# One level of Strassen's algorithm in both products of an FFN (hybrid decoder block, one Trainium2 core)

## The chip, the core and the metric

The kernel runs on one core of a Trainium2 chip. The core has TensorE (PE, matrix products, with PEld for its weight loads), VectorE (DVE), ScalarE (ACT), GpSimd (POOL) and SyncE (SP, which here issues every DMA). They run side by side, each through a queue of its own in a fixed order, and wait for one another by semaphores. SBUF is the working memory of 128 partitions; PSUM holds the sums of matmuls in eight banks of 128 x 512 float32. The metric is the device time in microseconds of one execution; lower is better.

## The reference

One layer of a hybrid decoder block on 1024 tokens of width 1024, with 16 meta tokens ahead of them, all in float32. Three mixers (sliding-window attention, forgetting attention, a gated recurrence) are merged and added to the residual `h`; the FFN follows. The change concerns the last four lines alone:

```python
u = rms_norm(h, norm_mix[l])
proj = u @ w_in[l]
...
merged = (g[:, :, 0] * (o_a @ w_branch[l, 0])
          + g[:, :, 1] * (o_f @ w_branch[l, 1])
          + g[:, :, 2] * (o_c @ w_branch[l, 2]))
h = h + merged @ w_out[l]
u = rms_norm(h, norm_ffn[l])
gate_ff, up_ff = jnp.split(u @ w_ffn_in[l], 2, axis=-1)      # 1024 -> 2 x 2816
h = h + (jax.nn.silu(gate_ff) * up_ff) @ w_ffn_out[l]        # 2816 -> 1024
return rms_norm(h, norm_final)[:, N_META:]
```

## The kernel before

Every large product is made of float32r matmuls in three passes. A float32 operand is split into a high part (`hi`, a copy on ACT into float32r) and the rest (`lo`, a subtraction on DVE): `split`, L115 to L124. `mm3` (L143) then multiplies hi by hi, hi by lo and lo by hi into one bank, so each 128 x 128 x 512 step is three matmuls.

The kernel is written with a tile framework. It finds the dependences between tiles by itself and sets the waits; a pool's `bufs` says how many tiles of a tag live at once, and a new tile of the tag waits until an old one is no longer read. A planner sets the order of the instructions on each engine ahead of time: of those that are ready in its model of the run it takes the one written first.

The projections, the mixers and their merging run first. Then the loop at L851 makes, for each half `c` of the tokens (512 tokens), `h` after the mixers (kept in DRAM as `h1s`), its norm, and by transposes on TensorE (L873) the feature-major split tiles `u2[c][k]` for the eight k-tiles of 128 features.

The FFN (L880 on) goes through its 22 feature tiles of 128 in pairs `f0`. For each tile the weights of gate and up are loaded and split (`load_w`, L126: `wr` to `wh` and `wl`), and for each token half two banks, `mm_g` and `mm_u`, are filled over eight k-tiles (L906). ACT takes the sigmoid (L909), DVE multiplies gate, sigmoid and up (L910, L911) and the product `sg` is split into `hl` (L912). The two rows of `w_ffn_out` are loaded (`for`) and split into `fh` and `fl` (L917). Then the pair is multiplied into the output: for each of the eight token tiles and each half of the 1024 columns, six matmuls into a bank (`tr_fo` or `sc_fo`, L932), which DVE adds to `acc[tt]` in SBUF (L936). So the second product follows each pair of feature tiles at once. With the last pair the sum of squares (L940), the gain on POOL (L943), the final norm (`finish`, L889, with `rstd_from`, L175) and the output follow tile by tile.

Of the kernel before, what the change touches and what calls it, by code (L numbers as in the profile page):

```python
# [16 lines left out]
P = 128  # L17
D = 1024
# [33 lines left out]
def hybrid_block(ctx, tc, h_in, w_in, w_v0, w_v1, w_bd, par, rows, gains, relt, onehot,  # L52
# [19 lines left out]
    pad(cp, 128)  # L72
# [70 lines left out]
    def mm3(ps, terms):  # L143

        n = 3 * len(terms)
        cost = ps.shape[-1] / 2.4 + 3
        i = 0
        for ah, al, bh, bl in terms:
            for a, b in ((ah, bh), (ah, bl), (al, bh)):
                pe.matmul(ps, a, b, start=i == 0, stop=i == n - 1)  # L150
                i += 1
            yield 3 * cost
# [602 lines left out]
    mp = ctx.enter_context(tc.tile_pool(name="m4", bufs=16, side="left", reuse_waits="tile"))  # L755
    bp = ctx.enter_context(tc.tile_pool(name="b4", bufs=8, side="right", reuse_waits="tile"))

    def hl_tile(pl):

        t = pl.tile([P, D], F32R, tag="m4", name=nm("hl"))  # L760
        return t[:, :512], t[:, 512:]

# [59 lines left out]
    mt = [[None] * KT for _ in range(2)]  # L822
    u2 = [[], []]
    with tc.tile_pool(name="r4", bufs=1, side="right", reuse_waits="tile") as r4:
# [26 lines left out]
        with tc.tile_pool(name="r4b", bufs=1, side="right", reuse_waits="tile") as r4b:  # L851
            for c in range(2):
                u2[c] = [hl_tile(mp if c else bp) for k in range(KT)]
                for tt in range(4 * c, 4 * c + 4):
# [14 lines left out]
                    for half in range(2):  # L869
# [4 lines left out]
                        for i in range(4):  # L874
                            k = 4 * half + i
                            split(u2[c][k][0][:, q], u2[c][k][1][:, q], pt[:, i * P:(i + 1) * P],
                                  part[:, P_NF + k:P_NF + k + 1])


    with tc.tile_pool(name="r5", bufs=1, side="right", reuse_waits="tile") as r5:  # L880
        acc = []
        for tt in range(8):
            a = r5.tile([P, D], F32, name=f"acc{tt}")
            dma(a, h1s[tt])
            acc.append(a)
        gfc = r5.tile([P, D], F32, name="gfc")
        dma(gfc, gains[1:2].partition_broadcast(P))

        def finish(tt, q, o):  # L889

            r = rstd_from(q, P)
            act.activation(o[0], o[0], AF.Copy, scale=r)
            dve.tensor_scalar(o[1], o[1], r, None, ALU.mult)  # L893
            for half in (1, 0):
                dma(out[tt * P:(tt + 1) * P, 512 * half:512 * half + 512], o[half])

        fin = {}
        for f0 in range(0, NF, 2):
            fow, at_ = [], []
            for f in range(f0, f0 + 2):  # L900
                w = [load_w(w_fi[f + NF * i], D) for i in range(2)]
                at_.append([hl_tile(mp) for c in range(2)])
                for c in range(2):
                    pg, pv = (mm_bank(f"_{x}{f}") for x in "gu")
                    for ps, (wh, wl) in zip((pg, pv), w):
                        run(mm3(ps, [(wh[:, k * P:(k + 1) * P], wl[:, k * P:(k + 1) * P], *u2[c][k])  # L906
                                     for k in range(KT)]))
                    sg = r5.tile([P, 512], F32, tag="sg", bufs=2, name=nm("sg"))
                    act.activation(sg, pg, AF.Sigmoid)  # L909
                    dve.tensor_tensor(sg, pg, sg, ALU.mult)  # L910
                    dve.tensor_tensor(sg, pv, sg, ALU.mult)  # L911
                    split(*at_[-1][c], sg)  # L912
                raw = wp.tile([P, D], F32, tag="wr", name=nm("for"))
                dma(raw, w_fo[f * P:(f + 1) * P])
                fh = r5.tile([P, D], F32R, tag="fh", bufs=3, name=nm("fh"))
                fl = r5.tile([P, D], F32R, tag="fl", bufs=3, name=nm("fl"))
                split(fh, fl, raw)  # L917
                fow.append((fh, fl))
            for tt in range(8):
                c, t0 = tt // 4, (tt % 4) * P  # L920
                q = slice(t0, t0 + P)
                last = f0 == NF - 2
                cols = [slice(0, 512), slice(512, D)]
                if last and tt == 7:
                    cols[1:] = [slice(512, 768), slice(768, D)]
                if last:
                    fin[tt] = (cp.tile([P, len(cols)], F32, tag=f"sf{len(cols)}", bufs=2, name=nm("sf")),
                               [r5.tile([P, 512], F32, tag="o", bufs=6, name=nm("o")) for _ in range(2)])
                for i, n in enumerate(cols):
                    w = n.stop - n.start  # L930
                    ps = (tr_bank, sc_bank)[i % 2](f"_fo{f0}")[:, :w]
                    run(mm3(ps, [(at_[i][c][0][:, q], at_[i][c][1][:, q], fow[i][0][:, n], fow[i][1][:, n])  # L932
                                 for i in range(2)]))
                    if last and tt > 0 and i == 1:
                        finish(tt - 1, *fin[tt - 1])
                    dve.tensor_tensor(acc[tt][:, n], ps, acc[tt][:, n], ALU.add)  # L936
                    if last:
                        sums, o = fin[tt]
# [82 lines left out]
```

## Time and profile before

| | us |
|---|---|
| median of 3 runs | 1741.51 (1741.38 to 1741.55) |
| the profiled execution | 1742.17 |
| its span, first to last instruction | 1740.4 |
| FFN in that span, first `mm_g` to last matmul | 1009.0 to 1729.75 |

How to read the rows that follow. The page's first part gives busy time, share of the span and number of instructions for each engine. A row of the windows view is one stretch of time: its length, the busy time of PE, PEld, DVE, ACT and POOL with instruction counts, the granted TensorE clock (1.00 is full speed), the share of the DMA engines in use and GB/s. A row of the groups view has line, engine, operation, what is written from what, partitions x elements and count, then the busy time in us and the mean length of one in ns, then the idle time before it and who ended it. A row of the timeline or of the chain of work begins with its start and length in us. Matmuls overlap in the pipeline, so the length of one is longer than the distance between two.

### The profile page before, as it was taken

What the parts mean: (1) busy time and instruction counts of PE and PEld (TensorE: products, weight loads), DVE (VectorE), ACT (ScalarE), POOL (GpSimd) and SP (SyncE); (2) the same over time, 40 slices, a digit from 0 to 9 for tenths busy, and PEclk for the clock granted to TensorE, in tenths of its full rate; (3) what the DMA queues carried; (4) which work ended last, traced back from release to release, by engine and by line L of the source; (5) the groups of instructions that cost most, each with busy time, mean ns of one, the idle gap of its engine ahead of it and who ended that gap; (6) DMA issues with size and microseconds to landing.
All of it is one profiled execution on the core that took longest, in us unless ns stands there. A gap on an engine that the chain in (4) does not pass through costs nothing.

```text
span 1740.4 us, 22250 instructions
## 1 busy us (share of the span) xinstructions
PE 1710.8 (98%) x8537; PEld 1443.1 (83%) x8537; DVE 865.9 (50%) x1746; ACT 647.2 (37%) x1228; POOL 192.4 (11%) x188
## 2 busy tenths in 40 slices
PE   7999999999999999999999999999999999999997
PEld 6898878888888888888878888888888888888885
DVE  6466565554666666513384344434434434434435
ACT  6455565554555555523364331211211211211214
POOL 2111011011222222102240000000000000000004
PEclk9999999999999999999999999999999999999999
DMA  7223242332432323197462241211211211211202
GB/s 259 67 94 109 103 126 98 104 100 70 140 103 73 121 68 111 61 325 261 139 224 97 85 169 37 73 37 37 73 37 37 73 37 37 73 37 37 73 12 97
DMA packets 70122, 170.35 MB, mean 98 GB/s; under 512 B 7416, under 2 KB 19016, under 8 KB 69760
## 3 DMA queue, kind: packets, MB, share of 16 engines
q1 hardware_dynamic: 70016, 168.93, 28.9%
q8 instruction: 67, 1.10, 0.3%
q14 instruction: 39, 0.32, 0.1%
HBM read 123.08 MB, written 40.49 MB: 94 GB/s over the span
## 4 chain that ended last, share of the span: by engine, by line
PE 85%; DVE 6%; issue 4%; ACT 2%; DMA 2%; POOL 1%; SPq 0%; POOLq 0%; DVEq 0%; ACTq 0%
PE mm_w L150 23%; PE mm_g L150 14%; PE mm_u L150 14%; PE sc_fo L150 6%; PE tr_fo L150 6%; PE mm_br L150 5%; PE mm_wo L150 5%; PE ob L547 3%; PE tr L558 3%; PE mm_v L150 2%; PE sc L632 1%; PE sc L633 1%; DVE o L893 1%; DVE x L400 1%; DVE wl L119 1%
## 5 line engine op out<-in xcount | busy, mean ns | idle before, releaser
L150 PE MATMUL mm_w<-uh,wh 128*128 128x512 f32 (+2 forms) x744 | 292.4, 393 | 0.0
L150 PE MATMUL mm_w<-uh,wl 128*128 128x512 f32 (+2 forms) x744 | 280.6, 377 | 0.0
L150 PE MATMUL mm_w<-ul,wh 128*128 128x512 f32 (+2 forms) x744 | 279.7, 376 | 0.0
L150 PE MATMUL mm_g<-hl,wh 128*128 128x512 f32 x704 | 217.0, 389 | 0.0
L150 PE MATMUL mm_u<-hl,wh 128*128 128x512 f32 x704 | 216.7, 389 | 0.0
L119 DVE TENSOR_TENSOR wl<-wr,wh 128x1024 fp32r<-128x1024 f32 x85 | 105.0, 1235 | 165.7 <-ACT wh L118 165.4
L118 ACT ACTIVATE wh<-wr 128x1024 fp32r<-128x1024 f32 x85 | 90.2, 1061 | 217.2 <-PE mm_g L150 81.9
L150 PEld LDWEIGHTS mm_w<-uh,wl 128*128 128x128 f32 x744 | 139.9, 188 | 25.5
L150 PEld LDWEIGHTS mm_g<-hl,wh 128*128 128x128 f32 x704 | 132.2, 188 | 27.6
L150 PEld LDWEIGHTS mm_u<-hl,wh 128*128 128x128 f32 x704 | 132.0, 188 | 27.3
L150 PEld LDWEIGHTS mm_w<-uh,wh 128*128 128x128 f32 x744 | 140.4, 189 | 12.7
L150 PEld LDWEIGHTS mm_w<-ul,wh 128*128 128x128 f32 x744 | 140.7, 189 | 11.7
L150 PE MATMUL mm_g<-hl,wl 128*128 128x512 f32 x352 | 136.9, 389 | 0.0
L150 PE MATMUL mm_u<-hl,wl 128*128 128x512 f32 x352 | 136.9, 389 | 0.0
L909 ACT ACTIVATE sg<-mm_g 128x512 f32<-128x512 f32 x44 | 26.0, 591 | 288.2 <-PE mm_g L150 288.2
L150 PE MATMUL tr_fo<-fh,hl 128*128 128x512 f32 (+1 forms) x356 | 123.5, 388 | 0.0
L150 PE MATMUL sc_fo<-fh,hl 128*128 128x512 f32 (+1 forms) x352 | 122.3, 388 | 0.8 <-DVE re L183 0.8
L150 PE MATMUL mm_br<-o,wh 128*128 128x512 f32 x384 | 118.3, 389 | 0.0
L119 DVE TENSOR_TENSOR pl<-tr,ph 128x384 fp32r<-128x384 f32 (+2 forms) x160 | 87.4, 555 | 47.1 <-ACT ph L118 43.1
L943 POOL TENSOR_TENSOR o<-acc,gfc 128x512 f32<-128x512 f32 x15 | 19.4, 1316 | 796.3 <-DVE acc L936 791.3
L911 DVE TENSOR_TENSOR sg<-mm_u,sg 128x512 f32<-128x512 f32 x44 | 30.4, 692 | 148.1 <-PE mm_u L150 148.1
L118 ACT ACTIVATE ph<-tr 128x384 fp32r<-128x384 f32 (+2 forms) x160 | 76.9, 486 | 52.9 <-PE tr L558 50.8
(207 smaller groups left out, 3161.3 us busy)
## 6 DMA issues: line engine op xcount, KB each, us to landing
wr<-w_in_dram SPq DMA_DIRECT2D x45, 512.0 KB, 3.7
wr<-w_fi_dram SPq DMA_DIRECT2D x44, 512.0 KB, 3.5
gz<-z SPq DMA_DIRECT2D x48, 256.0 KB, 2.1
o<-osp SPq DMA_DIRECT2D x24, 512.0 KB, 5.6
sg<-gz SPq DMA_DIRECT2D x48, 256.0 KB, 3.2
for<-w_fo_dram SPq DMA_DIRECT2D x22, 512.0 KB, 3.4
wb<-w_br_dram SPq DMA_DIRECT2D x24, 256.0 KB, 4.2
k<-k SPq DMA_DIRECT2D x20, 260.0 KB, 3.6
```

The costliest lines, as they stand in the source:

```text
L118: act.activation(hi, src, AF.Copy)
L119: i = dve.tensor_tensor(lo, src, f32(hi), ALU.subtract)
L150: pe.matmul(ps, a, b, start=i == 0, stop=i == n - 1)
L400: dve.tensor_tensor_scan(hs, r, g, 0.0, ALU.mult, ALU.add)
L547: pe.matmul(ob[:, q0:q0 + b - a], vt[:, c], x[:, a:b], start=count == 0, stop=count == n_mm - 1, skip_group_check=True)
L558: pe.transpose(tb[:, col:col + P], src, ident)
L632: pe.matmul(sc[:, :n], qs, kh[:, k0:k0 + n], start=True, stop=False)
L633: pe.matmul(sc[:, :n], qs, kl[:, k0:k0 + n], start=False, stop=True)
L893: dve.tensor_scalar(o[1], o[1], r, None, ALU.mult)
L909: act.activation(sg, pg, AF.Sigmoid)
L911: dve.tensor_tensor(sg, pv, sg, ALU.mult)
L943: pool.tensor_tensor(g, acc[tt][:, n], gfc[:, n], ALU.mult)
```

## The change

Strassen's algorithm, in Winograd's form, computes a 2 x 2 block product with 7 block products in place of 8, with sums of blocks as operands and of the products.

In the first product the blocks are: of the weights, gate and up of a feature tile by the two halves of the k-tiles (`a11`, `a12`, `a21`, `a22`); of the activations, the two halves of the k-tiles by the two token halves (`b11` to `b22`, now pairs of k-tiles in one tile). The sums of activations, T1 to T4, are made once by `combine()`; the sums of weights are made for each tile on POOL. Tile 0 is still computed by eight products (`swiglu_plain`). Some products are added onto a bank that holds an earlier one (`first=False`), after that one has been read.

In the second product the blocks are: token halves by feature tiles 0 to 10 and 11 to 21; and these by column halves of `w_ffn_out`. The first stage therefore takes tiles `j` and `j + 11` together, makes the sums on POOL (`combine_w`, `combine_a`) and writes the operands of the seven products to DRAM (`asp`, `bsp`). A second stage reads them back, splits them and runs the seven products one after the other, each over four banks.

```diff
-    def mm3(ps, terms):
+    def mm3(ps, terms, first=True):
...
-                pe.matmul(ps, a, b, start=i == 0, stop=i == n - 1)
+                pe.matmul(ps, a, b, start=first and i == 0, stop=i == n - 1, skip_group_check=not first)
...
+    def pair_tile(pl, **kw):
+        return [pl.tile([P, D], F32R, tag="m4", name=nm("pt"), **kw).rearrange("p (k t) -> p k t", k=2)
+                for a in range(2)]
...
-        for f0 in range(0, NF, 2):
...
-            for tt in range(8):
...
+        def product(ps, a, b, first=True):
+            run(mm3(ps, [(a[:, 0, k * P:(k + 1) * P], a[:, 1, k * P:(k + 1) * P],
+                          b[k // 2][0][:, k % 2], b[k // 2][1][:, k % 2]) for k in range(4)], first))
+
+        def operand(pl, tag, bufs, src):
+            t = pl.tile([P, 2, 512], F32R, tag=tag, bufs=bufs, name=nm(tag))
+            split(t[:, 0], t[:, 1], src)
+            return t
...
+        def swiglu(f, w, bb):
+            (a11, a12), (a21, a22) = w
+            b11, b21, b22, t1, t2, t3, t4 = bb
+            p1, p2, p5 = mm_bank(f"_s{f}"), sc_bank(f"_s{f}"), tr_bank(f"_s{f}")
+            g0, g1, u1 = (t5("c", 8) for _ in range(3))
+            s0, s1 = (t5("a", 6) for _ in range(2))
+            s2 = t5("s2", 2)
+            product(p1, operand(wp, "wh", 2, a11), b11)
+            act.activation(g0, p1, AF.Copy)
+            product(p2, operand(wp, "wl", 2, a12), b21)
+            add(dve, g0, p2, g0)
+            act.activation(s0, g0, AF.Sigmoid)
+            dve.tensor_tensor(s0, g0, s0, ALU.mult)
+            sub(pool, a21, a11, a21)
+            sub(pool, s2, a22, a21)
+            product(p1, operand(r5, "ar", 3, s2), t2, False)
+            act.activation(g1, p1, AF.Copy)
+            add(pool, a11, s2, a11)
+            product(p5, operand(r5, "ar", 3, a11), t1)
+            act.activation(u1, p5, AF.Copy)
+            product(p1, operand(r5, "ar", 3, a21), t3, False)
+            add(dve, u1, p1, u1)
+            sub(pool, a12, a12, s2)
+            product(p5, operand(wp, "wh", 2, a12), b22, False)
+            add(dve, g1, p5, g1)
+            act.activation(s1, g1, AF.Sigmoid)
+            dve.tensor_tensor(s1, g1, s1, ALU.mult)
+            dve.tensor_tensor(s1, u1, s1, ALU.mult)
+            product(p1, operand(wp, "wl", 2, a22), t4, False)
+            dve.tensor_tensor(s0, p1, s0, ALU.mult)
+            return [s0, s1]
+
+        def combine():
+            b11, b21 = u2[0][:2], u2[0][2:]
+            b12, b22 = u2[1][:2], u2[1][2:]
...
+            for k in (0, 2, 1, 3):
+                e = pool if k > 1 else dve
+                v3, v2[k] = t5("c", 8), t5("c", 8)
+                for v, x, y in zip((v3, v2[k]), parts(b22, k), parts(b12, k)):
+                    sub(e, v, x, y)
+                add(e, v3, v3, v2[k])
+                for x, y in zip((v3, v2[k]), parts(b11, k)):
+                    add(e, v2[k], x, y)
+                into(t2, k, v2[k])
+                into(t3, k, v3)
+            t4 = [pair_tile(mp) for _ in range(2)]
+            for t, b in ((t1, b22), (t4, b21)):
+                for k in (0, 2, 1, 3):
+                    e = pool if k > 1 else dve
+                    v = t5("c", 8)
+                    h, l = parts(b, k)
+                    sub(e, v, h, v2[k])
+                    add(e, v, v, l)
+                    into(t, k, v)
+            return b11, b21, b22, t1, t2, t3, t4
...
+        def combine_w(j):
+            raws = []
+            for i in range(2):
+                raw = t5("fo", 2, D)
+                dma(raw, w_fo[(j + NJ * i) * P:(j + NJ * i + 1) * P])
+                raws += halves(raw)
+            b11, b12, b21, b22 = raws
+            t2 = t5("t2", 1)
+            sub(pool, b12, b22, b12)
+            add(pool, t2, b12, b11)
+            sub(pool, b11, b22, t2)
+            sub(pool, b21, b21, t2)
+            for i, x in ((2, t2), (3, b11), (4, b12), (6, b21)):
+                dma(bsp[i][j], x)
+
+        def combine_a(j, a11, a21, a12, a22):
+            s2 = t5("t2", 1)
+            spill(1, j, a12)
+            spill(6, j, a22)
+            sub(pool, a21, a11, a21)
+            sub(pool, s2, a22, a21)
+            add(pool, a11, s2, a11)
+            sub(pool, a12, a12, s2)
+            for i, x in ((2, s2), (3, a11), (4, a21), (5, a12)):
+                spill(i, j, x)
+
+        for j in range(NJ):
+            if j == 0:
+                first = swiglu_plain(0)
+                ws = fetch_fi(NJ, 0)
+                bb = combine()
+            else:
+                first = swiglu(j, fetch_fi(j, 1), bb)
+                ws = fetch_fi(j + NJ, 0)
+            spill(0, j, first[0])
+            combine_w(j)
+            combine_a(j, *first, *swiglu(j + NJ, ws, bb))
...
+        def operands(i, j):
+            raw = wp.tile([P, 2, 512], F32, tag=("wr", "wh", "wl")[j % 3], bufs=2, name=nm("raw"))
+            dma(raw[:, 0], asp[i][j])
+            dma(raw[:, 1], right_operand(i, j))
+            t = rr.tile([P, 2, 2, 512], F32R, tag="ab", bufs=15, name=nm("ab"))
+            split(t[:, 0], t[:, 1], raw)
+            return t[:, 0], t[:, 1]
+
+        def product2(i, banks, first=True, by_token=None):
...
+            if by_token is None:
+                for j in range(NJ):
+                    ops = {j: operands(i, j)}
+                    for x in range(4):
+                        mm(x, ops, [j])
+            else:
+                ops = [operands(i, j) for j in range(NJ)]
+                for x in range(4):
+                    mm(x, ops, range(NJ))
+                    by_token(x)
...
+        product2(0, yb)
...
+        ho = [[h_tile(tt, half) for half in range(2)] for tt in range(8)]
+        for x in range(4):
+            add(dve, ho[x][0], yb[x], ho[x][0])
+        product2(1, xb)
...
+        product2(5, xb, False)
+        for x in range(4):
+            add(dve, ho[x][1], xb[x], ho[x][1])
+            total(x, 1)
+            finish(x)
+
+        def last(x):
+            add(dve, ho[4 + x][0], yb[x], ho[4 + x][0])
+            total(4 + x, 0)
+            finish(4 + x)
+        product2(6, yb, False, last)
```

`swiglu_plain` is the old loop's first product for one tile; `fetch_fi` loads the weights of gate and up without splitting them, into two buffers of one of two pools by turns; `spill` writes an operand to `asp`; `mm` in `product2` issues three matmuls for each `j` into the bank of token tile `x`; `total` and `finish` take the sum of squares, the norm and the output of a token tile.

More of the change, by code (lines that the diff above doesn't have):

```diff
@@ L71, in hybrid_block @@
     pad(edge, LINE - 32)
-    pad(cp, 128)
+    pad(cp, 192)
     ctxu = ctx.enter_context(ExitStack())
@@ L754, in hybrid_block @@
     ctxu.close()
-    mp = ctx.enter_context(tc.tile_pool(name="m4", bufs=16, side="left", reuse_waits="tile"))
-    bp = ctx.enter_context(tc.tile_pool(name="b4", bufs=8, side="right", reuse_waits="tile"))
+    ctx4 = ctx.enter_context(ExitStack())
+    mp = ctx4.enter_context(tc.tile_pool(name="m4", bufs=16, side="left", reuse_waits="tile"))
+    bp = ctx4.enter_context(tc.tile_pool(name="b4", bufs=8, side="right", reuse_waits="tile"))
     def hl_tile(pl):
@@ L852, in hybrid_block @@
             for c in range(2):
-                u2[c] = [hl_tile(mp if c else bp) for k in range(KT)]
+                u2[c] = [pair_tile(mp if c else bp) for k in range(KT // 2)]
                 for tt in range(4 * c, 4 * c + 4):
@@ L875, in hybrid_block @@
                             k = 4 * half + i
-                            split(u2[c][k][0][:, q], u2[c][k][1][:, q], pt[:, i * P:(i + 1) * P],
+                            split(*(x[:, k % 2, q] for x in u2[c][k // 2]), pt[:, i * P:(i + 1) * P],
                                   part[:, P_NF + k:P_NF + k + 1])
-    with tc.tile_pool(name="r5", bufs=1, side="right", reuse_waits="tile") as r5:
-        acc = []
-        for tt in range(8):
[L883 to L886, printed above, removed]
-        dma(gfc, gains[1:2].partition_broadcast(P))
[L889 to L897, printed above, removed]
-        for f0 in range(0, NF, 2):
[L899 to L938, printed above, removed]
-                        junk = r5.tile([P, 512], F32, tag="jk", bufs=2, name=nm("jk"))
-                        act.activation(junk[:, :w], acc[tt][:, n], AF.Square, accum_out=sums[:, i:i + 1])
-                        g = o[n.start // 512][:, n.start % 512:n.start % 512 + w]
-                        if w == 512:
-                            pool.tensor_tensor(g, acc[tt][:, n], gfc[:, n], ALU.mult)
-        for n in cols[1:]:
-            tc.keep_in_program_order(dve.tensor_tensor(o[1][:, n.start - 512:n.stop - 512], acc[7][:, n],
-                                                       gfc[:, n], ALU.mult))
-        finish(7, *fin[7])
```

88 lines of the change are left out of this document (added).

## The prediction

> **What bounds the kernel now.** I read the page's busy times first, then the busy time by stage for the FFN, then the groups of TensorE there, and last the chain of work.
>
> ```profile
> PE 1710.8 (98%) x8537; PEld 1443.1 (83%) x8537; DVE 865.9 (50%) x1746; ACT 647.2 (37%) x1228; POOL 192.4 (11%) x188
> 1009.00:1729.90 720.90, 719.95 (x3183) 595.44 (x3181) 292.47 (x398) 134.81 (x203) 16.13 (x13) 1.00 0.17 57
> L150 PE MATMUL mm_g<-hl,wh 128*128 128x512 f32 x704 | 217.0, 389 | 0.0
> L150 PE MATMUL mm_u<-hl,wh 128*128 128x512 f32 x704 | 216.7, 389 | 0.0
> L150 PE MATMUL mm_g<-hl,wl 128*128 128x512 f32 x352 | 136.9, 389 | 0.0
> L150 PE MATMUL mm_u<-hl,wl 128*128 128x512 f32 x352 | 136.9, 389 | 0.0
> L150 PE MATMUL tr_fo<-fh,hl 128*128 128x512 f32 x352 | 122.6, 389 | 0.0
> L150 PE MATMUL sc_fo<-fh,hl 128*128 128x512 f32 x348 | 121.4, 389 | 0.2 <-DVE re L183 0.2
> L150 PE MATMUL tr_fo<-fl,hl 128*128 128x512 f32 x176 | 68.5, 389 | 0.0
> L150 PE MATMUL sc_fo<-fl,hl 128*128 128x512 f32 x174 | 67.7, 389 | 0.0
> ...
> 1075.53 5.44 PE mm_g L150 x24
> ...
> 1140.81 5.44 PE mm_g L150 x24
> ```
>
> In the FFN (1009.0 to 1729.9 us) TensorE is busy 719.95 of 720.90 us while DVE needs 292 and ACT 135: TensorE alone sets the end. The groups give 2112 matmuls for the first product and 1050 full ones for the second, and twelve half-width ones make up the other 6: 3168 in all. The 389 ns are latencies of overlapping matmuls; the pace is the chain's, 24 in 5.44 us, **0.2267 us** each. A pair of feature tiles (288 matmuls) repeats after 1140.81 - 1075.53 = 65.28 us, the same pace, so there is no hole between groups. Full-width work is 3168 x 0.2267 = 718 us.
>
> **What the change removes.** A Strassen step does a feature tile's gate and up for both token halves in 7 products of 4 k-tiles x 3 passes, 84 matmuls, where the old loop has 2 x 2 x 8 x 3 = 96. Tile 0 stays plain: 96 + 21 x 84 = 1860, 252 fewer. The second product is 7 x 11 x 4 x 3 = 924 for 1056, 132 fewer. Together 384 x 0.2267 = **87.0 us**.
>
> The end of the old loop goes too.
>
> ```profile
> 1729.47 0.28 PE L150 MATMUL tr_fo<-fh,hl 128*128 128x256 f32 x1
> 1734.37 0.41 DVE L936 TENSOR_TENSOR acc<-tr_fo,acc 128x256 f32<-128x256 f32 x1
> 1734.88 0.42 ACT L940 ACTIVATE jk<-acc 128x256 f32<-128x256 f32 x1 [0.57 <-DVE acc L936]
> 1736.33 0.49 DVE L893 TENSOR_SCALAR o<-o,rs 128x512 f32<-128x512 f32 x1
> 1736.38 0.72 ACT L892 ACTIVATE o<-o,rs 128x512 f32<-128x512 f32 x1 [0.28 <-DVE rs L185]
> L873 PE MATMUL tr<-ident,xg 128*128 128x128 f32 x8 | 1.1, 276 | 0.0
> L119 DVE TENSOR_TENSOR hl<-sg,hl 128x512 fp32r<-128x512 f32 x44 | 30.3, 689 | 15.4 <-ACT hl L118 15.4
> L911 DVE TENSOR_TENSOR sg<-mm_u,sg 128x512 f32<-128x512 f32 x44 | 30.4, 692 | 148.1 <-PE mm_u L150 148.1
> L118 ACT ACTIVATE hl<-sg 128x512 fp32r<-128x512 f32 x44 | 27.5, 625 | 124.4 <-DVE sg L911 124.4
> L119 DVE TENSOR_TENSOR wl<-wr,wh 128x1024 fp32r<-128x1024 f32 x42 | 51.5, 1225 | 93.4 <-ACT wh L118 93.4
> L118 ACT ACTIVATE wh<-wr 128x1024 fp32r<-128x1024 f32 x42 | 44.6, 1063 | 162.7 <-PE mm_g L150 81.9 <-PE mm_u L150 80.8
> L943 POOL TENSOR_TENSOR o<-acc,gfc 128x512 f32<-128x512 f32 x15 | 19.4, 1316 | 796.3 <-DVE acc L936 791.3 <-issue 3.0 <-DMA out_dram<-o 1.0
> ```
>
> The last matmul ends at 1729.75 and the span at 1740.4: a tail of 10.65 us, since DVE had a backlog and reached the last bank 4.6 us late. Now each of the last four token tiles has 33 matmuls (7.5 us) to be finished under. Of the last one stands: the add 0.7, the square 0.6, from its end to the scaling about 1.0 (1734.88 + 0.42 to 1736.33), two scalings at 0.7, and the 3.3 us from the last scaling's end (1737.10) to the span's end: about 6.9, **3.8 us saved**. PE's old holes in the last groups were 720.75 - 718 - about 0.8 for the eight transposes, **1.8 us**, and go. With nothing added the span is 1740.4 - 87.0 - 3.8 - 1.8 = **1647.8**.
>
> **What it adds, stage by stage.** *First product, steady state.* A tile is 84 matmuls, 19.0 us. On ACT 7 hi halves, 3 bank copies and 2 sigmoids, about 12 x 0.6 = 7 us; on DVE 7 lo halves and 7 bank or gating operations, 14 x 0.69 = 9.7; on POOL 4 sums per tile and 8 more per pair for the second product's operands, 8 x 1.32 = 10.5. None reaches 19.0. New is that a product adds onto a bank which ACT or DVE is still to read (`first=False`): one product (2.72 us) always lies between, against a copy of 0.6 or an add of 0.7, so 2 us of queue in front of them are covered.
>
> But POOL and DVE are not independent.
>
> ```profile
> 905.10 2.86 POOL L843 TENSOR_TENSOR sg<-sg,macc 128x512 f32<-128x512 f32 x2 [3.30 <-DVE sg L842]
> 905.47 0.69 DVE L842 TENSOR_TENSOR sg<-mm_br,sg 128x512 f32<-128x512 f32 x1
> 907.41 1.10 DVE L119 TENSOR_TENSOR hl<-sg,hl 128x512 fp32r<-128x512 f32 x1 [1.25 <-ACT hl L118]
> 911.90 1.29 POOL L843 TENSOR_TENSOR sg<-sg,macc 128x512 f32<-128x512 f32 x1 [0.42 <-DVE sg L842]
> 912.51 1.23 DVE L119 TENSOR_TENSOR hl<-sg,hl 128x512 fp32r<-128x512 f32 x1 [0.69 <-ACT hl L118]
> ```
>
> DVE's lo half at 907.41 takes 1.10, not 0.69: POOL ends at 907.96, and 0.55 us later DVE ends too. At 912.51 again: POOL ends at 913.19, DVE at 913.74. DVE's read of a bank (905.47) isn't held up. So where both of DVE's inputs lie in SBUF it waits for POOL, and holds it off for some 0.55 us itself. [...]
>
> In a pair that is 16 POOL operations x 1.29 = 20.6 us and 20 such DVE ones (14 lo halves, 6 gatings) x 0.55 = 11.0: 31.6 of 38.1 us. It fits; bounds 0 and 20 us for the whole loop (the upper end worked out in the rivals). A product's DVE work is about two operations, 1.4 us, and 2.7 with a whole POOL operation ahead, just under its 2.72; so near the lower end: **3 us**.
>
> *The start.* `combine()` builds T1 to T4 from u2.
>
> ```profile
> 1018.37 0.61 DVE L124 SCALAR_TENSOR_TENSOR hl<-tr,part,hl 128x128 fp32r<-128x128 f32 x2 [0.18 <-ACT hl L123]
> ```
>
> u2 is whole at 1019.0. TensorE is covered by the plain tile until 1009.0 + 21.8 + 0.8 = 1031.6 and by the two products that need no T until 1037.0. T2 and T3 take 10 operations on POOL and 10 on DVE plus 8 lo halves. If the POOL ones and as many of DVE's alternate, 10 x (1.29 + 0.55) = 18.4, and the last split 1.3 and a wait: ready about 1040, 3 us late. T1 (4 and 4 operations, 7.4, its split behind) comes at 1046 against 1042.7: 4 us more. T4 at 1054 is just in time. If POOL and DVE didn't hold each other up, POOL's 10 x 1.29 would end at 1032 and nothing would wait; if all 42 us of port time (18 x 1.29 + 34 x 0.55) with DVE's bank work stood in line, some 18 are lost. Bounds 0 and 18; from the rows above I take **8 us**.
>
> ```profile
> 1732.00:1733.00 1.00, 0.00 (x0) 0.00 (x0) 0.54 (x3) 0.97 (x4) 1.00 (x2) 0.99 1.04 401
> 1733.00:1734.00 1.00, 0.00 (x0) 0.00 (x0) 1.00 (x2) 1.00 (x4) 1.00 (x1) 0.50 0.15 55
> 760.00:780.00 20.00, 20.00 (x90) 16.56 (x89) 1.86 (x2) 4.99 (x8) 0.00 (x0) 1.00 0.91 326
> for<-w_fo_dram SPq DMA_DIRECT2D x22, 512.0 KB, 3.4
> gz<-z SPq DMA_DIRECT2D x48, 256.0 KB, 2.1
> 914.90 0.33 SPq L58 DMA_DIRECT2D for<-w_fo_dram  x1
> ```
>
> The granted clock falls to 0.50 some 3.2 us after the last matmul, so a stall beyond that is paid with slow matmuls too; how long they stay slow no row shows. [...]
>
> *The DRAM path.* A pair loads 6 x 512 KB and spills 11 x 256 KB, 5.9 MB in 38.1 us, 154 GB/s; the second stage reads 512 KB per 12 matmuls (2.72 us), 193 GB/s. At 760 us the kernel moves 326 GB/s with TensorE fully busy, so both fit, with a landing of 2 to 4 us under six raw buffers (16 us ahead). In the second stage a step needs ACT 1.06 and DVE 1.23 of 2.72, and POOL is idle. The last product needs 11 operands at once, which the ring of 15 holds. All transfers are issued on SP, 17 in a pair at 0.33 us, and a spill that waits for its tile holds up the loads behind it; these are a tile (19 us) ahead, and that is their cover. The `h` rows and `gfc` are loaded under the first product of the second stage (44 steps, 30 us), where before they came at the FFN's start; u2's pair tiles hold the same columns, and I cost them at nothing.
>
> *The seam.* The first four ring slots lie where b11 and b21 were, free after the second product of the last tile, so 4 x 2.72 = 10.9 us are covered; the next may wait for the last `combine_a`: 0.7 + 2.1 spill + 1.3 + 2.1 spill + split 2.3, with issue gaps about 9. Bounds 0 and 9; covered, so **1 us**.
>
> Sum: 1647.8 + 3 + 8 + 1 = 1659.8 us span. The profiled execution took 1742.17 for 1740.4, 1.8 more, and lies 0.7 above the median 1741.51: **1661 us**.
>
> **Rivals.** *Nothing waits* (1649, chance 0.12): the planner starts sums early enough. For it: POOL is idle before 1019; against it: the rows of blocked splits.
>
> *The shared port becomes the bound* (about 1681, 0.18): if every POOL operation stands in DVE's way whole, DVE needs 28 x 0.69 + 20.6 = 39.9 us in a pair, over TensorE's 38.1, 1.9 x 10.5 = 20 us more than forecast. For it: both blocked rows; against it: 8 of DVE's 28 read banks and run beside POOL.
>
> *POOL waits in the order written* (slower, about 1758, 0.08): `combine_w` and `combine_a` stand ahead of the next tile's sums, and a waiting POOL operation holds those behind it. In the middle of a pair the path would be multiply 0.7, weight load 3.4, four sums 5.2, two of the next tile 2.6, split 1.3: 13.2 against two free products, 5.44; lost 7.8. At its end 0.7 + 2.1 + 1.3 + 2.6 + 1.3 = 8.0, lost 2.5. With 10.5 pairs 108 us, over the 93 saved; it decides from 8.8 us a pair on. Against it:
>
> ```profile
> 1053.58 1.06 ACT L118 ACTIVATE wh<-wr 128x1024 fp32r<-128x1024 f32 x1 [3.84 <-PE mm_u L150]
> 1054.55 1.05 ACT L118 ACTIVATE fh<-for 128x1024 fp32r<-128x1024 f32 x1
> 1055.50 0.62 ACT L118 ACTIVATE hl<-sg 128x512 fp32r<-128x512 f32 x1
> ```
>
> Both weight splits belong to feature tile 2 and run before tile 1's own `hl<-sg`, written earlier: engines follow a planned order by readiness, not the written one.
>
> **How the numbers follow.** Forecast (1653 to 1674) 0.55; nothing waits 0.12; port bound (1674 to 1695) 0.18; order as written 0.08; a mixture of stalls to 1738 0.05; within 0.2% 0.01; other slow causes 0.01. The range 1650 to 1690 leaves out the last four, a third of the first rival and the end of the second, 0.2 together. A measurement of this kernel can tell about 0.2% from no change. Faster 0.90, same 0.01, slower 0.09.
>
> **What would show it.** Matmuls in the page: 384 full ones fewer (8537 records, some 380 fewer), at the same 24 per 5.44 us. Waits of PE for `combine`'s tiles around 1037 to 1055 of some 8 us, none longer later; lo halves near 1.0 us in the first stage and 1.23 for 1024 columns in the second; the span's tail near 7 us. I am wrong if PE waits for POOL or for operand splits in every tile, if the pace of 0.2267 changes with the new operand layout, or if the ring waits for DMA.

## The result and the profile after

| | before | after |
|---|---|---|
| median, us | 1741.45 (1740.86 to 1741.55) | 1684.05 (1683.39 to 1686.76) |
| ratio, 95% interval | 1 | 0.9674 (0.9657 to 0.9691) |
| span of the profiled execution, us | 1740.4 | 1681.6 |

The changed kernel is faster by 57 us. The forecast was 1661: right in its sign and 23 us too low; the measured time lies inside the stated range, 1650 to 1690. The page of the changed kernel begins so:

```profile
PE 1628.9 (97%) x8147; PEld 1372.5 (82%) x8147; DVE 1003.4 (60%) x1815; ACT 766.0 (46%) x1413; POOL 463.8 (28%) x363
```

There are 390 matmul records fewer, as 384 fewer matmuls ask for. The removed work is gone; so something has been added on TensorE's path. These are a row of the chain of work in the middle of the first product (start, length, what) and then the windows (length, busy time of PE, PEld, DVE, ACT and POOL, granted clock, DMA share, GB/s):

```profile
1097.69 5.44 PE mm_s L150 x24
```

```profile
1030.00:1040.00 10.00, 1.09 (x5) 0.56 (x3) 6.33 (x6) 1.15 (x2) 9.77 (x7) 0.72 0.48 172
1040.00:1050.00 10.00, 1.22 (x2) 0.50 (x2) 8.19 (x7) 2.93 (x6) 8.36 (x6) 0.50 0.07 26
1050.00:1060.00 10.00, 6.00 (x16) 4.19 (x16) 10.00 (x10) 4.22 (x8) 7.64 (x5) 0.76 0.07 26
1060.00:1070.00 10.00, 5.97 (x17) 4.76 (x18) 9.38 (x12) 4.63 (x8) 3.80 (x3) 0.66 0.00 0
1100.00:1440.00 340.00, 340.00 (x1501) 281.59 (x1500) 224.34 (x249) 127.43 (x214) 215.32 (x142) 1.00 0.45 154
1510.00:1660.00 150.00, 150.00 (x663) 124.25 (x663) 87.07 (x97) 67.45 (x86) 0.00 (x0) 1.00 0.60 203
```

The pace is still 24 matmuls in 5.44 us. In the steady state of the first product TensorE is busy 340.00 of 340.00 us, in the second 150.00 of 150.00. All of the trouble lies in the 40 us after 1030, where TensorE is busy 14.28 of 40 us and its clock falls to 0.50. The waits of PE in the FFN (what waited, for what; us in total, times, longest) and their places on PE's timeline, where the bracket is the idle time ahead of the row:

```profile
PE mm_s L150 <- ACT wh L118: 12.7, 1, 12.7
PE mm_s L150 <- DVE wh L119: 5.9, 1, 5.9
PE sc_s L150 <- DVE wl L119: 5.4, 1, 5.4
PE sc_y L1082 <- DVE ab L119: 2.2, 1, 2.2
PE mm_s L150 <- ACT c L952: 1.7, 1, 1.7
PE mm_x L1082 <- DVE ab L119: 0.4, 1, 0.4
```

```profile
1008.07 0.62 PE L150 MATMUL mm_g<-pt,wh 128*128 128x512 f32 x2
...
1043.84 1.22 PE L150 MATMUL mm_s<-pt,wh 128*128 128x512 f32 x2 [12.74 <-ACT wh L118]
1050.96 4.36 PE L150 MATMUL mm_s<-pt,wh 128*128 128x512 f32 x10 [5.91 <-DVE wh L119]
...
1081.66 2.43 PE L150 MATMUL mm_s<-pt,wh 128*128 128x512 f32 x10
```

From the first matmul of the FFN (1008.07) to the end of the first Strassen tile (the next begins at 1081.66) pass 73.6 us. The work in them is 96 + 84 = 180 matmuls at 0.2267 and eight transposes, 41.6 us. So the start loses **32.0 us**: 25.7 in the four waits, and 6.3 beside them, most of it because matmuls run slowly after the longer waits (ten take 4.36 us at 1050.96, at a clock of 0.50 until 1054, where they take 2.43 at 1081.66). The rest of the span: 1647.8 of the forecast's floor, less 0.9 since the FFN begins at 1008.07 and not at 1009.0, plus 32.0, plus 2.6 in the two waits for `ab`, at the seam and 33 us behind it, is 1681.5 of 1681.6.

What PE waits for is a surprise. It isn't a T. `wh` and `wl` here are the split halves of `a11` and `a12`, the two weight operands whose products need no T at all, and `c` at L952 is a copy out of a bank. These are the timelines of ACT, DVE and POOL:

```profile
1037.94 1.15 ACT L118 ACTIVATE pt<-c 128x512 fp32r<-128x512 f32 x2 [12.49 <-POOL c L903]
1042.63 0.63 ACT L118 ACTIVATE pt<-c 128x512 fp32r<-128x512 f32 x1 [3.54 <-POOL c L903]
1043.17 0.61 ACT L118 ACTIVATE wh<-wr 128x512 fp32r<-128x512 f32 x1
```

```profile
1013.30 0.68 DVE L900 TENSOR_TENSOR c<-pt,pt 128x512 f32<-128x512 f32 x1
...
1021.86 1.77 DVE L903 TENSOR_TENSOR c<-c,pt 128x512 f32<-128x512 f32 x1
1023.56 1.77 DVE L119 TENSOR_TENSOR pt<-c,pt 128x512 fp32r<-128x512 f32 x1
1025.25 0.68 DVE L930 TENSOR_TENSOR a<-mm_u,a 128x512 f32<-128x512 f32 x1
...
1064.50 2.97 DVE L119 TENSOR_TENSOR pt<-c,pt 128x512 fp32r<-128x512 f32 x3
```

```profile
1021.35 1.74 POOL L900 TENSOR_TENSOR fo<-fo,fo 128x512 f32<-128x512 f32 x1
1023.04 1.74 POOL L903 TENSOR_TENSOR c<-c,pt 128x512 f32<-128x512 f32 x1
...
1026.56 3.32 POOL L900 TENSOR_TENSOR fo<-fo,t 128x512 f32<-128x512 f32 x2
```

ACT stands idle for 12.49 and 3.54 us before splits of the combination (`pt<-c`), because POOL hasn't made their sums; the split `wh<-wr` that PE waits for stands behind them in ACT's fixed queue and runs at once when they are done. The sums are late, for one thing, because DVE and POOL take turns: while both read SBUF, one operation of each takes 1.70 us (1021.86 to 1023.56 on DVE, 1021.35 to 1023.04 on POOL), where DVE alone needs 0.68; a DVE operation that reads a bank (1025.25) keeps its 0.68. For another, POOL makes five sums of weights between 1024.74 and 1033.24, before it goes on with the combination's own: of the second product's weights (`fo<-fo,t` among them) and of the first Strassen tile's (`wr<-wr,wr` at 1029.84, `s<-wr` at 1031.65). The combination lasts from 1013.30 to the last split's end at 1067.47, 54.2 us. (The recorded texts speak of a port where the turns are taken; the rows show the turns and their lengths, not where they arise.)

The end of the span, by the timeline:

```profile
1674.81 0.69 DVE L903 TENSOR_TENSOR h<-tr_y,h 128x512 f32<-128x512 f32 x1 [3.80 <-PE tr_y L1082]
```

The last bank is read at 1674.81, at once, and the span ends 6.8 us later.

### The profile page after: what moved, and what is told of

Read it like the earlier page. It is cut to its first block, busy times and chain, and to the rows that moved or that the text cites. A ratio compares the mean times of both kernels' runs of the same rounds, so it can differ in the third digit from the quotient of the medians.

```text
span 1681.6 us, 22693 instructions
## 1 busy us (share of the span) xinstructions
PE 1628.9 (97%) x8147; PEld 1372.5 (82%) x8147; DVE 1003.4 (60%) x1815; ACT 766.0 (46%) x1413; POOL 463.8 (28%) x363
## 4 chain that ended last, share of the span: by engine, by line
PE 80%; DVE 7%; issue 4%; DMA 4%; ACT 3%; POOL 2%; SPq 0%; POOLq 0%; DVEq 0%; ACTq 0%
PE mm_w L150 23%; PE mm_s L150 13%; PE tr_s L150 7%; PE mm_br L150 5%; PE mm_wo L150 5%; PE mm_x L1082 4%; PE sc_s L150 4%; PE ob L547 3%; PE tr L558 3%; PE tr_y L1082 3%; PE sc_y L1082 3%; PE mm_v L150 2%; PE ob_x L1082 1%; PE sc L632 1%; PE sc L633 1%
## 5 line engine op out<-in xcount | busy, mean ns | idle before, releaser
L119 DVE TENSOR_TENSOR ab<-raw,ab 128x1024 fp32r<-128x1024 f32 x77 | 95.9, 1262 | 62.6 <-ACT ab L118 60.2
L150 PE MATMUL mm_s<-pt,ar 128*128 128x512 f32 x504 | 121.3, 389 | 1.7 <-ACT c L952 1.7
L118 ACT ACTIVATE ab<-raw 128x1024 fp32r<-128x1024 f32 x77 | 80.9, 1059 | 88.4 <-DMA raw<-w_fo_dram 29.2
L118 ACT ACTIVATE wh<-wr 128x1024 fp32r<-128x1024 f32 (+1 forms) x85 | 71.7, 845 | 97.1 <-PE mm_w L150 50.6
L150 PEld LDWEIGHTS mm_s<-pt,ar 128*128 128x128 f32 x504 | 94.5, 188 | 21.6 <-ACT c L952 2.1
L150 PEld LDWEIGHTS mm_br<-o,wh 128*128 128x128 f32 x384 | 72.0, 188 | 15.3 <-ACT wh L118 0.3
L150 PE MATMUL mm_s<-pt,wh 128*128 128x512 f32 x252 | 63.4, 401 | 18.6 <-ACT wh L118 12.7
L558 PE MATMUL tr<-ident,s 128*128 128x128 f32 x480 | 79.6, 274 | 1.2 <-POOL s L596 0.6
L150 PE MATMUL mm_wo<-woh,hl 128*128 128x512 f32 x256 | 79.1, 390 | 0.0
L150 PE MATMUL mm_br<-o,wl 128*128 128x512 f32 x192 | 75.3, 392 | 1.8 <-DVE wl L119 1.6
```

The source lines that it names most:

```text
L118: act.activation(hi, src, AF.Copy)
L119: i = dve.tensor_tensor(lo, src, f32(hi), ALU.subtract)
L150: pe.matmul(ps, a, b, start=first and i == 0, stop=i == n - 1, skip_group_check=not first)
L558: pe.transpose(tb[:, col:col + P], src, ident)
```

## The experiments

**Theory.** The start's loss comes from the combination's length (18 sums on POOL, 18 sums and 16 splits on DVE, made longer by the turns of the two engines, 1.70 us for one operation of each, and by POOL's weight sums), against which the plain tile and two free products are too short a cover. **Rivals:** that it is the amount of work alone and the turns have no part in it; that it is the order in the queues alone, so that moving the few operations that PE needs ahead of the combination's would win the loss back; that something else in the first stage makes it. Times are medians; the kernel before took 1740.9 to 1741.9 beside each group of runs.

### Without the combination

```diff
-            if j == 0:
-                first = swiglu_plain(0)
...
+            first = swiglu_plain(j)
+            second = swiglu_plain(j + NJ)
```

All 22 tiles are plain here; only the second product is Strassen's.

> All 22 tiles of the first product are plain: no combined activations, no sums of its weights; only the second product is by Strassen's algorithm. The start's loss belongs to the combination, so it must be gone whole, while 12 matmuls a tile come back in 21 tiles: 252 x 0.2267 = 57.1 us. From the changed kernel's 1681.6: -31.8 (start) +57.1 = 1706.9 us of span, about 1709 on the clock. Both theories, turns at the port and order of the queues, say this. If a loss of over 5 us stays near 1008 to 1082 (time over 1714), it isn't the combination that makes it; if the time is under 1704, the second product gains more than its matmuls.

Measured 1713.76 us, ratio 0.9845 (0.983 to 0.9859), span 1710.7. One of its windows:

```profile
1040.00:1050.00 10.00, 10.00 (x45) 8.29 (x45) 2.52 (x3) 1.54 (x2) 0.00 (x0) 1.00 0.13 36
```

The hole at 1030 to 1070 is gone. This kernel leaves out the sums of weights and all else of the Strassen tiles with the combination; but the later Strassen tiles have all that too and lose nothing (340.00 of 340.00 us), so the hole belongs to the combination. The span is 3.8 us over the expected 1706.9, and 3.0 of these are waits for `ab` at the seam and just behind it, 5.6 us in all instead of 2.6. Set beside the changed kernel, the first product by Strassen's algorithm alone gives 29.7 us net (1713.76 to 1684.05, these 3.0 included) of the 57.1 that its 252 matmuls are worth.

### Less beside the combination, or fewer engines for it

`combine_w(0)`, with its sums on POOL, is written with the second pair:

```diff
-            combine_w(j)
+            if j == 1:
+                combine_w(0)
+            if j:
+                combine_w(j)
```

> The first combine_w is made with the second pair, so POOL's four sums of w_ffn_out are out of the start; no arithmetic changes. 'Turns': each of these stood between combine's operations (1021 to 1029 and 1043.8) and took 1.7 us at the ports: T's come 6 to 7 us earlier, 1677 (1672 to 1681). If POOL's place in the start doesn't matter (rival: the weight halves on ACT and DVE are late on account of the planned order alone): 1684 within 2.

Measured 1679.86 us, ratio 0.9649 (0.9635 to 0.9664): 4.2 us come back, inside what was expected but near its small end (1672 to 1681). The same four waits are there, the first of them 8.4 us for 12.7.

The combination's sums all on DVE:

```diff
-                e = pool if k > 1 else dve
+                e = dve
```

> All 52 operations of combine() on DVE, none on POOL. Now the start of the FFN costs 31.8 us over its matmuls (TensorE waits 25.7, the rest is slow clock). Theory 'turns': POOL and DVE take turns at the SBUF ports (1.70 us for a pair of operations in the changed kernel's trace) and the planned order doesn't reckon with it; then DVE alone, at 0.6 us each, needs 31 us where the two now need from 1013 to 1067: DVE's operations fall back from 1.77 to 0.69 us except beside POOL's six weight sums, the start costs 8 to 15 us, the kernel takes about 1664 (1658 to 1670). Rival 'work': the two engines are simply given too much, and each is independent of the other; then taking POOL's half away doubles DVE's share and the time is the same or worse: 1684 to 1695.

Measured 1679.62 us, ratio 0.9646 (0.963 to 0.9662). DVE has POOL's 18 sums to do besides its own 18, and the kernel is 4.4 us faster. The four waits of PE have become one. PE's timeline, and DVE's:

```profile
1055.87 4.63 PE L150 MATMUL mm_s<-pt,wh 128*128 128x512 f32 x10 [22.70 <-DVE wh L119]
```

```profile
1026.01 1.77 DVE L903 TENSOR_TENSOR c<-c,c 128x512 f32<-128x512 f32 x1
1027.70 0.68 DVE L900 TENSOR_TENSOR c<-pt,pt 128x512 f32<-128x512 f32 x1
...
1055.14 0.68 DVE L119 TENSOR_TENSOR wh<-wr,wh 128x512 fp32r<-128x512 f32 x1
```

Beside POOL's weight sums a DVE sum still takes 1.77 us (1026.01); when these are done it takes 0.68. The combination is over by 1057.0 and not by 1067.5. But the half that PE needs stands at 1055.14, behind nearly all of it, so neither number expected was met: the combination became 11 us shorter and 4.4 of these were won.

### More cover

The second tile, 11, is plain too: 12 matmuls (2.7 us) more, and 21.8 us more of work that needs no T.

```diff
                 first = swiglu_plain(0)
-                ws = fetch_fi(NJ, 0)
+                second = swiglu_plain(NJ)
                 bb = combine()
```

> Feature tile 11 is plain too, so TensorE has 21.8 us more that needs no sum, for 12 more matmuls (2.7 us). Both theories expect that what remains of combine() after the cover counts: the sums end at 1067 now; the cover ends at 1008.2 + 0.8 + 43.5 = 1052.5, with two products more 1057.9. 'Turns': tile 1's first products still find their weight halves queued behind combine's on ACT and DVE, so some 5 us are lost: 1684 - 31.8 + 2.7 + 5 = 1660 (1656 to 1666). A rival, 'the first product that adds onto a used bank stalls whatever comes ahead of it' (the bank has to be read first), expects the loss to move with the first Strassen tile and stay: 1684 + 2.7 = 1687.

Measured 1676.30 us, ratio 0.9628 (0.9613 to 0.9642): 7.8 us gained, a third of what cover alone should have given. The longest wait of PE:

```profile
PE mm_g L150 <- ACT wh L118: 13.2, 1, 13.2
```

It lies in a plain tile: the new cover's own weight halves stand behind the combination's splits. Then both edits together, and both with the sums on DVE alone; these two kernels ran side by side and differ only in that engine:

> Two plain tiles, and the first sums of the second product's weights written with the second pair, so that POOL has only the combination and the second pair's own weight sums. Lines of queue (what PE needs stands behind the combination's operations on ACT and DVE): the gains of the two edits made singly, -7.8 and -4.2, overlap, because the later weight sums now matter behind a cover that is 2.7 us longer: 1672 (1669 to 1675). Work alone (the amount between 1008 and 1082 sets the end): the two add up whole, 1672 less the 2.7 us that are already in the first of them, 1670. Nothing gained beside the two plain tiles alone (1676) would say that POOL's weight sums do not hold the second plain tile's weight halves.

> As the two plain tiles with the later weight sums, but the combination's sums all on DVE. Turns at the port: a sum on DVE beside one on POOL takes 1.7 us for the pair, and two on DVE alone take 2 x 0.68 = 1.36, so DVE alone ends sooner: the same as the kernel with both engines or up to 6 us faster, and DVE's sums fall to 0.68 throughout. Independent engines: DVE takes over some 26 sums of 0.68 to 1.0 us, 18 to 26 us more on the engine that also splits PE's weights, so it is 8 us slower or more than with both engines.

Measured 1671.27 us (ratio 0.9601, 0.9586 to 0.9615) with both engines, and 1665.07 us (0.9565, 0.9551 to 0.9579) with DVE alone. The first is as expected, though 1672 and 1670 lie too close together to tell the queue from the work; the second is 6 us faster, where engines that don't disturb each other would have made it slower: by 8 us or more in the expectation, which counts 26 sums moved where there are 18, and by about 11 with 18 sums 0.60 us apart. DVE's timeline, first with both engines and then with DVE alone, from the first sum to the last split:

```profile
1013.24 0.68 DVE L900 TENSOR_TENSOR c<-pt,pt 128x512 f32<-128x512 f32 x1
...
1034.43 1.75 DVE L900 TENSOR_TENSOR c<-pt,c 128x512 f32<-128x512 f32 x1
...
1068.41 1.28 DVE L119 TENSOR_TENSOR pt<-c,pt 128x512 fp32r<-128x512 f32 x2
```

```profile
1013.54 0.68 DVE L900 TENSOR_TENSOR c<-pt,pt 128x512 f32<-128x512 f32 x1
...
1031.05 0.68 DVE L903 TENSOR_TENSOR c<-c,pt 128x512 f32<-128x512 f32 x1
...
1055.52 1.89 DVE L119 TENSOR_TENSOR pt<-c,pt 128x512 fp32r<-128x512 f32 x3
```

With the 18 sums moved onto DVE the combination is done in 43.9 us (to 1057.41) instead of 56.4 (to 1069.69). The sums that POOL took over were no help but a brake. This decides for the turns and against the rival that the two engines work independently and only the amount counts.

### Other places in the order

Three edits move what PE needs ahead of the combination. First, the halves of `a11` and `a12` are split before it, in tiles of their own:

```diff
                 ws = fetch_fi(NJ, 0)
+                pre = [operand(r5, "ar", 3, x) for x in ws[0]]
                 bb = combine()
```

> The halves of the two weight operands that need no T (a11 and a12 of the first Strassen tile) are made before combine(), in buffers of another tag; combine() and everything else as in the changed kernel. TensorE's four waits at the start are for these halves (12.7, 5.9, 5.4) and one bank copy (1.7). 'Queue': these waits cost what they say, because the halves stand behind combine's operations on ACT and DVE; with them early TensorE goes on to 1036 without a hole, then waits for T2 (complete at about 1046 now), T1 (1057) and T4 (1067), so that 1684 falls to 1673 (1667 to 1678). If the sums were in time and only the queue was wrong, all of the 31.8 goes: 1653. If the sums alone set the end: 1684 within 2.

Measured 1685.66 us, ratio 0.9682 (0.9667 to 0.9696): nothing gained. PE's timeline, and ACT's:

```profile
1030.77 2.88 PE L150 MATMUL mm_s<-pt,ar 128*128 128x512 f32 x12
...
1058.91 1.22 PE L150 MATMUL mm_s<-pt,ar 128*128 128x512 f32 x2 [22.54 <-ACT c L952]
```

```profile
1058.26 0.60 ACT L952 ACTIVATE c<-mm_s 128x512 f32<-128x512 f32 x1 [1.45 <-POOL c L900]
```

The two free products now run without a hole, and the loss has moved whole to the next thing that PE needs: the copy of the first one's bank, which ACT makes at 1058.26, 24.6 us after that product's end (1033.65). By the bracket it waited last for a POOL sum of tag `c`; the combination's sums and these copies share that tag's eight buffers. Whether the copy is late by its place in ACT's queue or for want of a buffer, no run separates: a tag of its own for the copies wasn't tried.

Second, in the kernel with two plain tiles, later weight sums and both engines (1671.27), the second plain tile's weight halves get tiles of their own:

```diff
+            if f:
+                w = [load_own(w_fi[f + NF * i], *(("ar", 3), ("fo", 2))[i]) for i in range(2)]
```

> As the two plain tiles with the later weight sums, but the second plain tile's weight halves have tiles of their own and are split without waiting for the first tile's to come free. Queue: the second tile's 13 us wait of PE for these halves goes, and PE reaches the first Strassen tile with the combination further on: 1664 to 1668. Work alone: the combination ends when it did, PE waits for it one tile later, and the time is that of the kernel without the edit, within 2 us.

Measured 1680.32 us, ratio 0.9654 (0.9637 to 0.967), 9 us slower than without the edit. The waits of PE, and the longest of them with what leads to it on PE's and POOL's timelines:

```profile
PE mm_u L150 <- DVE a L939: 10.0, 2, 5.1
PE mm_s L150 <- DVE c L903: 7.8, 2, 6.5
```

```profile
1110.13 4.86 PE L150 MATMUL mm_s<-pt,wl 128*128 128x512 f32 x12 [6.50 <-DVE c L903]
```

```profile
1100.04 1.29 POOL L900 TENSOR_TENSOR fo<-fo,fo 128x512 f32<-128x512 f32 x1 [8.54 <-DMA fo<-w_fo_dram]
...
1106.44 1.26 POOL L903 TENSOR_TENSOR wr<-s,wr 128x512 f32<-128x512 f32 x1
```

The wait for the halves is gone; at the start PE waits 10.0 us for DVE's multiplications instead, which free its banks. That nearly cancels: the second Strassen tile begins at 1087.15, where it begins at 1086.74 without the edit. The rest of the 9 us arises at 1110, at the end of that tile, from a wait of 6.5 us and slow matmuls behind it, and is a side effect: the edit puts one weight's halves into the two `fo` buffers, so the rows of `w_ffn_out` are loaded late, POOL stands waiting for them (8.54 us), and the Strassen tile's own weight sum (`wr<-s,wr`) stands behind in POOL's queue. ACT, DVE and PE wait for that sum in turn.

Third, `combine()` is written inside the first Strassen tile, behind the two free products and what follows on them (`bb` is empty until then); once as it is, once with the sums on DVE and the later weight sums, and once with two plain tiles besides:

```diff
             dve.tensor_tensor(s0, g0, s0, ALU.mult)
+            if not bb:
+                bb.extend(combine())
+            b22, t1, t2, t3, t4 = bb[2:]
```

> The changed kernel with one thing else: combine() is written inside the first Strassen tile, behind the first two products, their bank copy and the sigmoid, which need no T. Queue: those two products run at 1030 to 1036 without a hole and nothing that they need stands behind a combination's operation; what is left is the wait for the T's themselves, which came complete at 1046 (T2), 1057 (T1) and 1067.5 (T4) in the changed kernel, so the tile can end 11 us sooner than at 1081.7: span 1670 (1667 to 1674). Work alone: the combination ends as late as before and PE with it, wherever it is written, as where only the two operands were split early: 1681 to 1685.

> One plain tile, combine() written inside the first Strassen tile, its sums on DVE alone, and the first sums of the second product's weights later. Queue and turns together: DVE ends the combination near 1057, as with two plain tiles, PE waits for T's alone, some 10 us, and 3 us of slow clock: floor 1647.0 + 2.2 (seam) + 13 = 1662 (1659 to 1667). If the place in the order does nothing: the kernel with the combination on DVE (1678.1) less the later weight sums (4.2), 1674.

> Two plain tiles, later weight sums, sums on DVE, and combine() written inside the first Strassen tile. Against the same kernel with combine() ahead of that tile (1664.6, of which 12.7 us lost at the start, by 1647.8 - 0.8 + 2.7 + 2.2 + 12.7): PE comes to the first T at 1058, when the combination is done at about 1057 to 1060. Queue: 0 to 4 us lost, 1652 to 1656. If the loss only moves on: 1662 to 1666.

Measured 1687.84 us (ratio 0.9692, 0.9678 to 0.9707), 1677.97 (0.9637, 0.9622 to 0.9651) and 1693.64 (0.972, 0.9704 to 0.9736). All three miss what the queue theory expected; the last is 28 us slower than the same kernel with `combine()` ahead of the tile. DVE's timeline of the first and the third:

```profile
1033.91 5.12 DVE L900 TENSOR_TENSOR c<-pt,pt 128x512 f32<-128x512 f32 x3
...
1078.68 1.88 DVE L119 TENSOR_TENSOR pt<-c,pt 128x512 fp32r<-128x512 f32 x3
```

```profile
1050.61 0.69 DVE L119 TENSOR_TENSOR wh<-wr,wh 128x512 fp32r<-128x512 f32 x1 [5.19 <-ACT wh L118]
...
1058.57 5.15 DVE L900 TENSOR_TENSOR c<-pt,pt 128x512 f32<-128x512 f32 x3
```

The combination now begins at 1033.9 and at 1058.6 instead of 1013, though its inputs haven't moved and DVE stands idle in between. On DVE's timeline its sums follow without a gap upon the splits of the Strassen tile's own weights, and these began late: in the third kernel `wh<-wr,wh` waited 5.19 us for ACT's half, and ACT's half 10.05 us for PE's matmuls of a plain tile, whose weight halves have the same tag. Read so, the block now stands behind these splits in DVE's queue; why the planner put it there stays open. These kernels gave up the cover that they were to use, and they don't test the order by itself. They do show its length once more: 46.7 us in the first (to 1080.56), 35.9 in the second (1034.23 to 1070.16 on its DVE timeline, with the weight sums later too).

### The combination under three plain tiles

The two tiles of the first pair and the first of the second pair are plain, and `combine()` is written behind them; its sums are on DVE, the first weight sums later:

```diff
+            elif j == 1:
+                first = swiglu_plain(1)
+                ws = fetch_fi(1 + NJ, 0)
+                bb = combine()
```

> Three plain tiles, combine() written behind the third, its sums on DVE, the first weight sums of the second product later. Cover against length: the combination took 36 us on DVE alone when it was written inside the first Strassen tile (1034.2 to 1070.2) and 44 us among other work with two plain tiles (1013.5 to 1057.3); PE now comes to the first Strassen tile at 1074. So 0 to 3 us are lost at the start, for 12 more matmuls (2.7 us): 1647.0 + 2 x 2.7 + 2.2 (seam) + 0 to 3 = 1655 to 1658, some 7 to 9 below the 1664.6 of the best so far. If the loss moves on with the operations that PE needs, wherever the cover ends: 1664.6 + 2.7 = 1667 or more.

Measured 1661.07 us (1660.46 to 1662.14), ratio 0.9538 (0.9522 to 0.9554), span 1659.9: the fastest of all, 23 us under the changed kernel. The waits of PE at the start, and the window with the seam:

```profile
PE mm_s L150 <- ACT c L952: 1.6, 1, 1.6
PE mm_s L150 <- ACT c L960: 0.5, 1, 0.5
```

```profile
1440.00:1480.00 40.00, 38.32 (x162) 31.62 (x163) 24.29 (x21) 17.07 (x17) 4.90 (x3) 0.96 0.97 359
```

TensorE works through the combination, on DVE, without a hole. 2.1 us of waits are left of the 25.7 at the start, for 5.4 us of matmuls put back. The span is 2 us above the upper end expected; the mean clock of 0.96 in the 40 us with the seam, 1.6 us, had not been reckoned with. (The seam's wait of 2.2 us is as long in the changed kernel, where the clock from 1455 to 1465 stayed at 1.00.)

## Why the prediction was right in sign and 23 us low

The measured 1684 lies above the forecast's own interval (1653 to 1674) and in that of the rival of the port as the bound (1674 to 1695), whose loss of 20 us in the steady state didn't come. That the stated range held is luck in part: the start lost 24 us more than forecast, and the stage for which the range had been left wide lost nothing.

- **The work removed (87.0 us): right.** 390 records fewer and the pace of 24 in 5.44 us unchanged, with the new layout of the operands.
- **The tail (6.9): right**, 6.8 measured.
- **Steady state of the first product (3, bounds 0 to 20): 0 measured.** Turns do happen there. One of DVE's groups between 1082 and 1462:

```profile
L119 DVE TENSOR_TENSOR wl<-wr,wl 128x512 fp32r<-128x512 f32 x39 | 40.4, 1037 | 1.1
```

  A lo half of 512 columns takes 1.04 us here and 0.88 to 1.26 in the three other groups, where "near 1.0" was forecast, and an addition out of a bank 0.69. But DVE is busy only 224 of 340 us, so the turns fit beside TensorE. The rival of the port as the bound falls for this stage: no trace shows every POOL operation in DVE's way whole, and these lo halves are on average 0.2 to 0.6 us longer than 0.69, beside POOL sums of 1.3 to 1.7 us. The turns that it was worked out from cost time at the start instead.
- **The start (8, bounds 0 to 18): 32.0 measured. This step failed, in size and in its upper bound.** It had the last T whole at 1054; the combination's last split ended at 1067.47. The turns were sized well (1.70 us for 1.84). What was left out: that the splits on DVE take turns with POOL too (1.77 us at 1023.56), where beside ten turns only the last split was counted; POOL's sums of weights between the combination's own (4.2 us for `combine_w(0)`, by the run that puts it later, and the first Strassen tile's besides); that the two free products and the plain tile's second half need splits, sigmoids and copies from the very queues in which the combination stands, so that the cover "by the two products that need no T until 1037.0" didn't hold; and the slow matmuls behind the waits (most of 6.3). The bound of 18 put 42 us of the two engines' operations and DVE's bank work in line, and the combination took 48.5 us from 1019.0 on; what broke the bound is that it still counted that cover whole.
- **How the clock was weighed.** The prediction had read one fall, to 0.50 some 3.2 us after the last matmul, and no row for how long matmuls then stay slow; its sum has nothing for slow matmuls. The changed kernel's trace has four stalls and shows it: the clock is at 0.50 from 1035 to 1054, under the stalls of 12.7 and 5.9 us and the matmuls behind them, and at 1.00 again from 1055, some 4 us after the matmuls of 1050.96 begin; the two between these stalls, at 1043.84, didn't bring it back. After the stall of 1.7 us it is still 1.00; under that of 5.4 us it falls to 0.50 and is 1.00 from 1069, some 5 us after the matmuls of 1064.03 begin. These slow matmuls are most of the 6.3 us.
- **The seam (1, bounds 0 to 9): 2.6.** 2.2 of these are a wait for a split in DVE's queue.
- **The DRAM path: as worked out, but for the `h` rows.** 154 GB/s in the first stage and 203 in the second (154 and 193 forecast). The loads of the `h` rows, costed at nothing, did hold up the ring: from 1475 to 1495 the DMA engines are busy throughout (404 to 405 GB/s), and ACT waits 9.33 us, to 1492.81, for a load of `raw` that is issued behind them. The ring covered it but for PE's 0.4 us wait for `ab` at 1495.
- **POOL in the order written: refuted for this kernel.** `fo<-fo` and `fo<-fo,t` of `combine_w`, written later, run in the midst of the combination from 1021 to 1030, and no tile of the steady state waits. The wait itself can happen: in the run with tiles of their own it cost 6.5 us once, when the rows for POOL's sums came late.

What is shown of the start: the hole is the combination's (its absence fills it), its length is set in part by the turns (43.9 us on DVE alone against 56.4 on two engines), and more cover and less length bring 23 us back together. What is only read from the trace: that the single operation for which PE waits is late by its place in a queue (or, for the bank copy, by a shared buffer). Moving that operation alone never paid: at the start PE then waited as long for another one behind the same block. How much the order by itself is worth stays open.

## What to carry to other kernels

A block of sums that is made once ahead of a loop has to be costed as a stage: its length on the engines that carry it, against the matmuls that cover it, with everything that TensorE needs from those engines in the meantime counted as standing behind it. DVE and POOL weren't two engines for these sums, which read both inputs from SBUF: half of them on POOL made the whole 12.5 us longer (56.4 for 43.9). When a freed wait turns up at the next operation behind the same block, that block is the bound: shorten its work or put more cover over it, don't move one operation.

## What wasn't expected of the hardware

The turns aren't fair in every case. In two of the kernels POOL hardly gets in while DVE runs two-input operations with no gap. POOL's timeline of the second kernel with `combine()` inside the tile, sums on DVE:

```profile
1039.31 18.39 POOL L900 TENSOR_TENSOR wr<-wr,wr 128x512 f32<-128x512 f32 x1 [5.55 <-DMA wr<-w_fi_dram]
1057.78 1.59 POOL L900 TENSOR_TENSOR s<-wr 128x512 f32<-128x512 f32 x1
```

One sum, 1.59 us for its neighbour, is shown as 18.39, while DVE makes 28 operations at their undisturbed 0.60 us apart; in the third of these kernels such a sum is shown as 24.50. Spans on POOL are rough, but its next sum doesn't start before 1057.78 either. In the changed kernel, where POOL and DVE each have operations waiting, they alternate at 1.70 us (1020 to 1025). Such turns don't explain an operation kept out for 18 us, over 28 of the other engine's. What decides between the two cases wasn't tried.
